# Subtractions with a higher priority, a scan whose vector and scalar instructions keep program order, and steps spread over more slots

## The chip, the cores and the metric

The kernel runs on one core of a Trainium2 chip. The metric is the device time of one execution in microseconds (us). Engines are named as in the profile: PE (matmul; PEld is its loading of weights), DVE (vector), ACT (scalar), POOL, SP (here it only issues DMAs).

## The reference

Two layers of a mixer over 256 tokens of 2048 features, in float32. One input projection feeds two groups of heads; both are gated and go through one output projection.

```
for l in range(DEPTH):
    h = rms_norm(x, norm_g[l])
    proj = jnp.einsum('btd,dc->btc', h, w_in[l])
    rw_in, g_rw, q, k_at, v_at, g_at = jnp.split(proj, col_splits, axis=-1)
    rw_in = bidir_token_shift(rw_in, shift_mu[l])
    r, k, v, xw, xa = jnp.split(rw_in, rw_splits, axis=-1)
    y_rw = rwkv7_branch(r, k, v, xw, xa, w0[l], decay_up[l], ...)
    ...                                   # rope on q and k
    y_at = window_attention(qh, kh, vh, sink[l])
    mix = concatenate([y_rw * silu(g_rw), y_at * silu(g_at)])
    x = x + jnp.einsum('btc,cd->btd', mix, w_out[l])
return rms_norm(x, final_g)
```

`rwkv7_branch` is a recurrence over time with a 64x64 state per head, run forward and backward for 16 heads, followed by a normalisation per head. `window_attention` has 16 heads over 4 key heads and a band of 128 tokens.

## The kernel before

**The matrix products.** Weights come as tiles of 128 x 1024 (half of 2048 rows times 128 output columns). `wload` (L205) issues one DMA into a `raw` buffer, of which there are three. `wsplit` (L210) makes two tiles of it, in two halves of 512 columns each: ACT copies raw to `hi` in the matmul's rounded format (L215), then DVE computes `lo = raw - hi` (L216). `hi` and `lo` have two buffers each. A `gemm` (L273 to L275) has 16 steps, eight a tile, each of three matmuls: activations' high part times `hi` (L273), their low part times `hi` (L274), their high part times `lo` (L275). `Stream.run(n)` issues n such steps, and asks for the next weight tile two steps before the last one ends. When a product is complete, an evacuation runs (`shift_evac` L400 to L403, `silu_evac` L411 to L413, rope L495 to L501).

**The recurrence.** Heads go in eight pairs p. Each pair passes three Python generators, which issue a part of their work at every `yield`:

- `scan_p` prepares: decays and rates through tanh (L645, L648), a scan along time (L658), exponentials `pp` and `ip` (L664, L665), a reciprocal of the key norm (L667), and the tiles `mv` (L675, L676, L690) and `bk` (L684, L687).
- `scan_i` makes and inverts a triangular matrix: a product masked into `ge` (L726), a half-precision copy `AB` (L735) and its remainder `AL` (L766), then six levels of products whose results are merged into `tv` and `tt` under a mask (L824, L825, for levels 1 to 5). Key rows are copied over a part of `ge` at L773.
- `scan_b` runs four steps along time: products into `pcc` (L870 from the second step on, L883, L893), an ACT copy to `suv` (L888), a DVE product into `suv` (L895). Its tail normalises over DVE, ACT and POOL (L911 to L915), and `mix_split` (L613) makes the high and low parts `MH`, `ML` of the result.

**What sets the order.** `window(64, ...)` cuts 64 gemm steps into 14 slots. In each slot the generators advance first, as the lists `STAGE_P`, `STAGE_I`, `STAGE_B` say (slot numbers; a number that stands twice means two advances), then four or five gemm steps are issued. Twelve windows make up most of a layer. In window w, `scan_p` works on pair w-1, `scan_i` on w-2 and w-3, `scan_b` on w-3 and w-4, so windows 3 to 8 have all three at once. Values of the attention are projected in window 8, keys and queries (rope) from window 9 on.

On PE the order is that of the program (L136). DVE, ACT and SP are ordered by a scheduler, which takes among the instructions that its own model holds ready the one of highest priority; priority falls in the order in which the code issues, and `scan_b` stands 95 places ahead (`PRIO_B`). Each engine then runs its list strictly in order.

**Buffers.** PSUM gives two tiles of two banks to all the scans' products (`wpair`), two banks to the gemms (`pm`), and one each to `pcc` and `py`.

Of the kernel before, what the change touches and what calls it, by code (L numbers as in the profile page):

```python
# [21 lines left out]
T = 256  # L22
# [15 lines left out]
NSH = 26  # L38
# [17 lines left out]

# [72 lines left out]
def hybrid_trunk_kernel(ctx, tc, xT, wi, wv, wo, par, fing, dup, iup, sink, pos, cst, out):  # L129
# [17 lines left out]
    def wpair(name):  # L147

        return ps_w.tile([128, 2, 512], F32, tag="w", name=name)
# [55 lines left out]
    def wload(src):  # L205
        raw = wrp.tile([128, 1024], F32, tag="raw", name="raw")
        SY.dma_start(out=raw, in_=src)
        return raw

    def wsplit(raw):  # L210
        hi = wsp.tile([128, 1024], F32R, tag="hi", name="hi")
        lo = wsp.tile([128, 1024], F32R, tag="lo", name="lo")
        for i in range(2):
            q = slice(i * 512, (i + 1) * 512)
            A.activation(hi[:, q], raw[:, q], AF.Copy)  # L215
            V.tensor_tensor(lo[:, q], raw[:, q], hi[:, q].bitcast(F32), op=ALU.subtract)  # L216
        return hi, lo

    def halves(src, first=None):
        return [lambda: wsplit(first if first is not None else wload(src[0])), lambda: wsplit(wload(src[1]))]  # L220

    class Stream:

# [383 lines left out]
    def layer(l):  # L607
# [21 lines left out]
                PE.matmul(o[r, 0:T], bones[r, r], x[r, 0:T], start=True, stop=True)  # L629


        def scan_p(p, t):
            K, VV, R, iu, du = t["k"], t["v"], t["r"], t["iu"], t["du"]
            dd = lambda x: x.rearrange("p (d x) -> p d x", d=2)
            two = lambda x: x.unsqueeze(1).to_broadcast([128, 2, T])
            c8 = lambda x: x.rearrange("p (n j) -> p n j", j=64)

            pza = wpair("pza")
            pz, pa = pza[:, 0], pza[:, 1]
            for d in range(2):  # L640
                low_rank(pz[:, d * T : (d + 1) * T], [a[0 : RANK + 1, d, :] for a in du], [a[0 : RANK + 1] for a in L.TW])
# [3 lines left out]
            A.activation(LW, pz, AF.Tanh, scale=0.5)  # L645
            TH = st("th", [2 * T])
            for d in range(2):
                A.activation(TH[:, d * T : (d + 1) * T], pa[:, d * T : (d + 1) * T], AF.Tanh, scale=0.5, bias=dpm(NSH + 16, d * 8 + p))  # L648
            sq = st("t1", [T], bufs=3)
            A.activation(sq, K, AF.Square, scale=prm(P_KK, p))  # L650
            KR = st("kkr", [T])
            A.activation(KR, K, AF.Identity, scale=prm(P_KK, p))
            yield

            V.tensor_scalar(LW, LW, 1.0, None, op0=ALU.add)
            msk = MSK.rearrange("p c j -> p (c j)")
            for x in (LW[:, 0:T], LW[:, T : 2 * T][:, ::-1]):
                V.tensor_tensor_scan(x, msk, x, 0.0, op0=ALU.mult, op1=ALU.add)  # L658
# [5 lines left out]
            A.activation(PP.rearrange("p d c j -> p (d c j)"), LW, AF.Exp, scale=DECAY_C)  # L664
            A.activation(IP.rearrange("p d c j -> p (d c j)"), LW, AF.Exp, scale=-DECAY_C)  # L665
            KD = st("kd", [T])
            V.reciprocal(KD, pk[:, 0:T])  # L667
            V.scalar_tensor_tensor(KD, KD, 1e24, KR, op0=ALU.min, op1=ALU.mult)
# [6 lines left out]
            V.scalar_tensor_tensor(MV[:, 0, :, 0, 1:64], PP[:, 0, :, 0:63], -1.0, kr4[:, :, 1:64], op0=ALU.mult, op1=ALU.mult)  # L675
            V.scalar_tensor_tensor(MV[:, 1, :, 0, 0:63], PP[:, 1, :, 1:64], -1.0, kr4[:, :, 0:63], op0=ALU.mult, op1=ALU.mult)  # L676
            A.activation(MV[:, 0, :, 0, 0:1], kr4[:, :, 0:1], AF.Copy, scale=-1.0)
            A.activation(MV[:, 1, :, 0, 63:64], kr4[:, :, 63:64], AF.Copy, scale=-1.0)
            A.activation(km, TH, AF.Identity, scale=dpm(NSH, p), bias=dpm(NSH + 8, p))
            yield  # L680
            V.scalar_tensor_tensor(dd(TH), dd(TH), 1.0, two(KD), op0=ALU.add, op1=ALU.mult)
            BK8 = BK.rearrange("p d c s j -> p (d c) s j")
            IP8 = IP.rearrange("p d c j -> p (d c) j")
            V.scalar_tensor_tensor(BK8[:, :, 1, :], c8(TH), 0.5, IP8, op0=ALU.mult, op1=ALU.mult)  # L684
            yield
            V.tensor_tensor(dd(km), dd(km), two(K), op=ALU.mult)
            V.tensor_tensor(BK8[:, :, 2, :], c8(km), IP8, op=ALU.mult)  # L687
            A.activation(BK8[64:128, :, 0, :], BK8[64:128, :, 2, :], AF.Copy)
# [5 lines left out]
            A.activation(PC[:, 0, :], PP[:, 0, :, 63], AF.Copy)  # L694
            A.activation(PC[:, 1, :], PP[:, 1, :, 0], AF.Copy)
            yield


            V.tensor_tensor(km[:, 0:T], km[:, 0:T], km[:, T : 2 * T], op=ALU.add)
            V.scalar_tensor_tensor(km[:, 0:T], km[:, 0:T], prm(P_RK, p), R, op0=ALU.mult, op1=ALU.mult)  # L700
            yield
            pb = wbank("pbn")
            head_sums(pb, km)
            bv = st("bv", [T], bufs=3)
            V.tensor_tensor(bv, pb[:, 0:T], VV, op=ALU.mult)
            t.update(BK=BK, MV=MV, PC=PC, bv=bv)
            yield


        def scan_i(p, t):  # L710
# [48 lines left out]
            for h in range(2):  # L759
                for q in range(2):  # L760
# [1 line left out]
                        pick(SUV, half[1 - h], q * 128 + h * 64, [NC * 128, 2], [256, 2], [1, 64]),  # L762
                        pts[h][half[q], 384:512].rearrange("p (b x) -> p b x", b=2).unsqueeze(1).to_broadcast([64, 2, 2, 64]), AF.Copy,
                    )
            for h in range(2):
                V.tensor_tensor(  # L766
                    flat(AL[half[h]]), GE[h][half[h]].rearrange("p d c s j -> p (d c) s j")[:, :, 0, :], flat(AB[half[h]]), op=ALU.subtract
                )


            for h in range(2):
                c3 = lambda x: pick(x, half[h], 0, [NC * 128 - 128, 2], [128, 3], [1, 64])
                A.activation(c3(GE[h][:, 0, 1:NC].rearrange("p c s j -> p (c s j)")), c3(MV[:, 0, 1:NC].rearrange("p c s j -> p (c s j)")), AF.Copy)  # L773

# [17 lines left out]
            for li, b in enumerate(LEVELS):  # L792
# [61 lines left out]
        def scan_b(p, t):  # L854
# [288 lines left out]
```

## Time and profile before

| | |
|---|---|
| time, three runs | 1252.38, 1253.78, 1256.28 us (median 1253.78) |
| profiled execution | 1253.19 us, span of the profile 1251.3 us |
| granted PE clock, mean | 0.993 of full speed |
| PE busy | 1186.6 us (95%), 16204 instructions |
| DVE busy | 928.8 us (74%), 2067 instructions |
| ACT busy | 747.3 us (60%), 1838 instructions |
| POOL busy | 19.0 us, 23 instructions |

The times are of unprofiled executions, the profile is of a further one. The trace can be asked for one engine's instructions in order of time; each row has the start and the length in us, the engine, the line, the operation, output and inputs with their shapes, and in brackets how long the engine stood idle ahead of it and what released it. `[0.84 <-ACT suv L888]` on a PE row says that PE stood for 0.84 us, until the ACT instruction that writes `suv` at L888 was done. Views by waits and by lines add such rows up. DVE lists its masked copies at L824 and L825 as CAST_PREDICATED in the trace and as COPY_PREDICATED in the program.

### The profile page before, as it was taken

What the parts mean: (1) busy time and instruction counts of PE and PEld (TensorE: products, weight loads), DVE (VectorE), ACT (ScalarE), POOL (GpSimd) and SP (SyncE); (2) the same over time, 40 slices, a digit from 0 to 9 for tenths busy, and PEclk for the clock granted to TensorE, in tenths of its full rate; (3) what the DMA queues carried; (4) which work ended last, traced back from release to release, by engine and by line L of the source; (5) the groups of instructions that cost most, each with busy time, mean ns of one, the idle gap of its engine ahead of it and who ended that gap; (6) DMA issues with size and microseconds to landing.
All of it is one profiled execution on the core that took longest, in us unless ns stands there. A gap on an engine that the chain in (4) does not pass through costs nothing. (4 is left out here: it accounts for less than half of the span.)

```text
span 1251.3 us, 38155 instructions
## 1 busy us (share of the span) xinstructions
PE 1186.6 (95%) x16204; PEld 1094.6 (87%) x16204; DVE 928.8 (74%) x2067; ACT 747.3 (60%) x1838; POOL 19.0 (2%) x23
## 2 busy tenths in 40 slices
PE   6989999999999999999999999999999999999996
PEld 6978888888888889999998888888888888899996
DVE  7878878887886668856676878878887766786654
ACT  6556665666566566645555655665666565665553
POOL 0000000000000000000000000000000000000000
PEclk9999999999999999999999999999999999999998
DMA  7443233322323434466654433223322333335663
GB/s 246 158 141 124 96 103 109 103 83 102 120 86 97 135 110 141 140 216 230 202 186 141 135 124 116 89 92 110 103 92 92 118 107 124 134 132 173 209 192 119
DMA packets 60411, 166.72 MB, mean 133 GB/s; under 512 B 7728, under 2 KB 22736, under 8 KB 60240
## 3 DMA queue, kind: packets, MB, share of 16 engines
q1 hardware_dynamic: 60240, 164.27, 39.9%
q8 instruction: 127, 2.08, 0.7%
q14 instruction: 44, 0.36, 0.1%
HBM read 157.43 MB, written 4.19 MB: 129 GB/s over the span
## 5 line engine op out<-in xcount | busy, mean ns | idle before, releaser
L273 PE MATMUL pm<-XH,hi 128*128 128x256 f32 x1664 | 495.9, 298 | 13.9 <-ACT XH L178 6.4
L275 PE MATMUL pm<-XH,lo 128*128 128x256 f32 x1664 | 470.6, 283 | 20.0 <-DVE lo L216 19.9
L274 PE MATMUL pm<-XL,hi 128*128 128x256 f32 x1664 | 468.6, 282 | 0.1
L215 ACT ACTIVATE hi<-raw 128x512 fp32r<-128x512 f32 x560 | 326.7, 624 | 201.6 <-PE pm L274 163.1
L216 DVE TENSOR_TENSOR lo<-raw,hi 128x512 fp32r<-128x512 f32 x560 | 367.8, 685 | 104.1 <-ACT hi L215 95.7
L273 PEld LDWEIGHTS pm<-XH,hi 128*128 128x128 f32 x1664 | 314.5, 189 | 40.0 <-issue 13.0
L275 PEld LDWEIGHTS pm<-XH,lo 128*128 128x128 f32 x1664 | 315.1, 189 | 25.7 <-DVE lo L216 25.6
L274 PEld LDWEIGHTS pm<-XL,hi 128*128 128x128 f32 x1664 | 315.0, 189 | 0.8 <-DVE XL L179 0.8
L273 PE MATMUL pm<-MH,hi 128*128 128x256 f32 x512 | 144.8, 283 | 1.6 <-ACT hi L215 1.6
L275 PE MATMUL pm<-MH,lo 128*128 128x256 f32 x512 | 144.6, 282 | 0.4 <-DVE lo L216 0.4
L274 PE MATMUL pm<-ML,hi 128*128 128x256 f32 x512 | 144.5, 282 | 0.0
L273 PEld LDWEIGHTS pm<-MH,hi 128*128 128x128 f32 x512 | 97.4, 190 | 2.6 <-ACT hi L215 1.8
L275 PEld LDWEIGHTS pm<-MH,lo 128*128 128x128 f32 x512 | 97.3, 190 | 0.6 <-DVE lo L216 0.6
L274 PEld LDWEIGHTS pm<-ML,hi 128*128 128x128 f32 x512 | 97.3, 190 | 0.0
L888 ACT ACTIVATE suv<-pcc 64x128 f32<-64x128 f32 x128 | 34.4, 269 | 16.2 <-PE pq L815 10.9
L968 ACT ACTIVATE mv<-mv,mx 128x257 f32<-128x257 f32 x64 | 31.9, 503 | 16.3 <-DVE mx L965 16.2
L726 DVE TENSOR_TENSOR ge<-pg,C 128x1024 f32<-128x1024 f32 x32 | 39.0, 1218 | 3.0 <-PE pg L720 3.0
L735 ACT ACTIVATE AB<-ge 64x512 f16<-64x512 f32 x32 | 20.1, 629 | 30.9 <-DVE ge L726 30.5
L720 PE MATMUL pg<-mv,bk 64*128 64x128 f32 x512 | 37.2, 285 | 0.0
L824 DVE CAST_PREDICATED tv<-LV,pd 128x256 f16<-128x256 uint8 x80 | 34.1, 426 | 1.7 <-PE pd L823 1.2
L817 ACT ACTIVATE QF<-pq 128x256 f16<-128x256 f32 x80 | 30.9, 386 | 6.9 <-PE pq L815 5.9
L825 DVE CAST_PREDICATED tt<-LV,pd 128x256 f16<-128x256 uint8 x80 | 34.0, 424 | 0.0
(240 smaller groups left out, 1843.6 us busy)
## 6 DMA issues: line engine op xcount, KB each, us to landing
raw<-wi SPq DMA_DIRECT2D x207, 512.0 KB, 3.4
raw<-wo SPq DMA_DIRECT2D x64, 512.0 KB, 3.3
raw<-wv SPq DMA_DIRECT2D x8, 512.0 KB, 3.2
rrot<-u SPq DMA_DIRECT2D x80, 32.0 KB, 1.9
vg<-xT SPq DMA_DIRECT2D x16, 128.0 KB, 4.1
xd<-vg SPq DMA_DIRECT2D x16, 128.0 KB, 3.3
vg<-xd SPq DMA_DIRECT2D x16, 128.0 KB, 3.3
g<-dup SPq DMA_DIRECT2D x16, 97.0 KB
```

Of the source, the lines that this page charges most:

```text
L215: A.activation(hi[:, q], raw[:, q], AF.Copy)
L216: V.tensor_tensor(lo[:, q], raw[:, q], hi[:, q].bitcast(F32), op=ALU.subtract)
L273: PE.matmul(pm, wh, rh[:, kk, :], start=(kk == 0), stop=False)
L274: PE.matmul(pm, wh, rl[:, kk, :], start=False, stop=False)
L275: PE.matmul(pm, wl, rh[:, kk, :], start=False, stop=(kk == 15))
L720: PE.matmul(pg[:, h, c * 128 : (c + 1) * 128], BK[half[h], d, c, 1 - h : 3 - h, :].rearrange("p s j -> p (s j)"), MV[half[h], d, c].rearra ...
L726: V.tensor_tensor(GEd(d), pg.rearrange("p h (c x) -> p h c x", c=NC), gm[d].unsqueeze(1).unsqueeze(1).to_broadcast([128, 2, NC, 128]), op= ...
L817: A.activation(t_sub(QF), flat4(pq[:, :, 0:128]), AF.Copy)
L824: V.copy_predicated(t_sub(TC), t_mask, flat4(pd[:, :, 0:128]))
L825: V.copy_predicated(v_sub(TT), v_mask, flat4(pd[:, 0, 128:384].rearrange("p (d x) -> p d x", d=2)))
L888: A.activation(here(h), pc[half[h], 1], AF.Copy)
L968: A.activation(Sc[:, h, q, 0:257], Sc[:, h, q, 0:257], AF.Exp, scale=0.125, bias=mx[:, q : q + 1], accum_out=den[:, q : q + 1])
```

## The change

Five things are edited.

1. In `wsplit` the subtraction is issued with a priority 40 places higher (`PRIO_LO`).
2. A wrapper `InTurn` makes each instruction that is called through it keep its place in the program's order on its engine: it stays behind the instruction issued before it there. All of `scan_p`'s ACT and DVE instructions go through it (`PA`, `PV`), and in `scan_i` and `scan_b` the copies `AB`, `AL`, the key rows, and most of the tail.
3. In `scan_i` the two `AB` copies are issued after a `yield` instead of before it, so one slot later; `AL` and the key rows are issued at level 1 and level 2 of the inversion instead of before level 0, which with `STAGE_I` is slot 4 and slot 6 instead of slot 2.
4. `scan_b`'s tail: the product with the gate is written in place instead of into `mf`, and there are three more `yield`s.
5. The second list of `STAGE_B` grows from `[1]` to `[1, 2, 3, 4]`, so that the tail's steps fall into slots 1 to 4 of the next window.

```
-STAGE_B = (list(range(1, 14)), [1])
+STAGE_B = (list(range(1, 14)), [1, 2, 3, 4])
...
+PRIO_LO = 40
...
-            V.tensor_tensor(lo[:, q], raw[:, q], hi[:, q].bitcast(F32), op=ALU.subtract)
+            with tc.high_priority(offset=PRIO_LO):
+                V.tensor_tensor(lo[:, q], raw[:, q], hi[:, q].bitcast(F32), op=ALU.subtract)
...
+    class InTurn:
...
+        def __getattr__(self, name):
+            return lambda *a, **k: tc.keep_in_program_order(getattr(self.engine, name)(*a, **k))
+
+    PA, PV = InTurn(A), InTurn(V)
...
         def scan_p(p, t):
...
-            V.tensor_scalar(LW, LW, 1.0, None, op0=ALU.add)
+            PV.tensor_scalar(LW, LW, 1.0, None, op0=ALU.add)
...
             for h in range(2):
-                A.activation(flat(AB[half[h]]), GE[h][half[h]].rearrange("p d c s j -> p (d c) s j")[:, :, 0, :], AF.Copy)
-            yield
+                PA.activation(flat(AB[half[h]]), GE[h][half[h]].rearrange("p d c s j -> p (d c) s j")[:, :, 0, :], AF.Copy)
...
-            for h in range(2):
-                V.tensor_tensor(
-                    flat(AL[half[h]]), GE[h][half[h]].rearrange("p d c s j -> p (d c) s j")[:, :, 0, :], flat(AB[half[h]]), op=ALU.subtract
-                )
...
+            def low_rows():
+                for h in range(2):
+                    PV.tensor_tensor(
...
+            def key_rows():
...
                 pq = wpair("pq")
+                if li in (1, 2):
+                    (low_rows, key_rows)[li - 1]()
                 if li == 0:
...
-            V.tensor_tensor(ysq, py, yv.unsqueeze(2).to_broadcast([128, NC, 64]), op=ALU.mult)
+            PV.tensor_tensor(ysq, py, yv.unsqueeze(2).to_broadcast([128, NC, 64]), op=ALU.mult)
...
             A.activation(Zt, pz, AF.Identity, scale=prm(P_LG, p), bias=prm(P_LB, p))
-            V.tensor_tensor(Zt, Zt, bv, op=ALU.add)
-            mix_split(p, Zt, t["gr"])
+            yield
+            PV.tensor_tensor(Zt, Zt, bv, op=ALU.add)
+            PV.scalar_tensor_tensor(Zt, Zt, 0.5, t["gr"], op0=ALU.mult, op1=ALU.mult)
+            yield
+            PA.activation(MH[:, p, :], Zt, AF.Copy)
+            yield
+            PV.tensor_tensor(ML[:, p, :], Zt, MH[:, p, :].bitcast(F32), op=ALU.subtract)
             yield
```

The number of instructions stays as it was on every engine. PE's order does not change, nor POOL's; on SP two weight loads come behind the four small copies of a rope step in two places. What moves is the order on DVE and ACT. Three places of it follow, as the program's lists have them (line, operation, output and inputs, shape; x2 stands for two in a row). Lines of the changed kernel lie somewhat further down: L216 of before is L218, L215 is L216, L824 is L844, L888 is L908, L895 is L915, L400 to L403 are L413 to L416, and every instruction that goes through the wrapper is listed under the wrapper's own line, L231.

**ACT, slots 5 and 6 of a window with all three scans.** Names: `pp`, `ip` exponentials of `scan_p`, `suv` of `scan_b`, `ge<-mv` key rows. Before:

```order
L645 ACTIVATE lw<-pza 128x512
L648 ACTIVATE th<-pza,DP 128x256 x2
L664 ACTIVATE pp<-lw 128x512
L888 ACTIVATE suv<-pcc 64x2x64 x2
L665 ACTIVATE ip<-lw 128x512
L694 ACTIVATE pc<-pp 128x4
L695 ACTIVATE pc<-pp 128x4
L679 ACTIVATE lw<-th,DP 128x512
L215 ACTIVATE hi<-raw 128x512 x2
```

Now:

```order
L231 ACTIVATE lw<-pza 128x512
L231 ACTIVATE th<-pza,DP 128x256 x2
L231 ACTIVATE t_3813<-kr,PR 128x256
L231 ACTIVATE kkr<-kr,PR 128x256
L231 ACTIVATE ge<-mv 64x6x64
L908 ACTIVATE suv<-pcc 64x2x64 x2
L231 ACTIVATE ge<-mv 64x6x64
L216 ACTIVATE hi<-raw 128x512 x2
L837 ACTIVATE QF<-pq 128x2x32x4
L231 ACTIVATE pp<-lw 128x512
L231 ACTIVATE ip<-lw 128x512
```

The `suv` copies leave the place behind `pp` and now stand behind two small ACT instructions and one key-row copy; `pp` and `ip` come behind two `hi` copies and a merge copy.

**DVE, slots 6 to 8 of the same window.** `kd`, `th`, `bk` and `mv` are `scan_p`'s, `vg` and `u` an evacuation's, `tv` and `tt` `scan_i`'s. Before:

```order
L667 RECIPROCAL kd<-pk 128x256
L216 TENSOR_TENSOR lo<-raw,hi 128x512
L668 SCALAR_TENSOR_TENSOR kd<-kd,kkr 128x256
L400 TENSOR_TENSOR u<-pm,rb 128x256
L824 COPY_PREDICATED tv<-LV,pd 128x2x32x4
L825 COPY_PREDICATED tt<-LV,pd 128x2x32x4
L402 SCALAR_TENSOR_TENSOR vg<-u,PR,vg 128x255
L681 SCALAR_TENSOR_TENSOR th<-th,kd 128x512
L403 SCALAR_TENSOR_TENSOR vg<-u,PR,vg 128x255
L684 SCALAR_TENSOR_TENSOR bk<-th,ip 128x8x64
L216 TENSOR_TENSOR lo<-raw,hi 128x512 x2
L687 TENSOR_TENSOR bk<-lw,ip 128x8x64
```

Now:

```order
L231 SCALAR_TENSOR_TENSOR kd<-kd,kkr 128x256
L844 COPY_PREDICATED tv<-LV,pd 128x2x32x4
L845 COPY_PREDICATED tt<-LV,pd 128x2x32x4
L231 SCALAR_TENSOR_TENSOR mv<-pp,kkr 128x4x63
L415 SCALAR_TENSOR_TENSOR vg<-u,PR,vg 128x255
L231 SCALAR_TENSOR_TENSOR mv<-pp,kkr 128x4x63
L416 SCALAR_TENSOR_TENSOR vg<-u,PR,vg 128x255
L218 TENSOR_TENSOR lo<-raw,hi 128x512 x2
L231 SCALAR_TENSOR_TENSOR th<-th,kd 128x512
L231 SCALAR_TENSOR_TENSOR bk<-th,ip 128x8x64
```

The pair of `lo` comes ahead of `th` and `bk`; the two `mv` products, which stood ahead of slot 6's work, now stand here.

**DVE, slots 3 to 5 of window 9, layer 0, where rope is computed.** `u`, `rrot` and `iu` are the rope's. Before:

```order
L496 TENSOR_TENSOR u<-u,TW 128x256
L497 TENSOR_TENSOR rrot<-rrot,XA 128x256
L895 TENSOR_TENSOR suv<-pcc,pc 64x2x64
L498 TENSOR_TENSOR u<-u,rrot 128x256
L895 TENSOR_TENSOR suv<-pcc,pc 64x2x64
L216 TENSOR_TENSOR lo<-raw,hi 128x512
L501 TENSOR_TENSOR iu<-u,kr 128x256
```

Now:

```order
L509 TENSOR_TENSOR u<-u,TW 128x256
L510 TENSOR_TENSOR rrot<-rrot,XA 128x256
L845 COPY_PREDICATED tt<-LV,pd 128x2x64x2
L511 TENSOR_TENSOR u<-u,rrot 128x256
L218 TENSOR_TENSOR lo<-raw,hi 128x512
L915 TENSOR_TENSOR suv<-pcc,pc 64x2x64
L514 TENSOR_TENSOR iu<-u,kr 128x256
L231 TENSOR_TENSOR ML<-t_7134,MH 128x256
L915 TENSOR_TENSOR suv<-pcc,pc 64x2x64
L231 TENSOR_TENSOR AL<-ge,AB 64x512 x2
```

A masked copy, a `lo`, a rope product and the tail's `ML` come to stand among or ahead of the two `suv` products.

More of the change, by code (lines that the diff above doesn't have):

```diff
@@ L663, in scan_p @@
             IP = st("ip", [2, NC, 64])
-            A.activation(PP.rearrange("p d c j -> p (d c j)"), LW, AF.Exp, scale=DECAY_C)
-            A.activation(IP.rearrange("p d c j -> p (d c j)"), LW, AF.Exp, scale=-DECAY_C)
+            PA.activation(PP.rearrange("p d c j -> p (d c j)"), LW, AF.Exp, scale=DECAY_C)
+            PA.activation(IP.rearrange("p d c j -> p (d c j)"), LW, AF.Exp, scale=-DECAY_C)
             KD = st("kd", [T])
-            V.reciprocal(KD, pk[:, 0:T])
-            V.scalar_tensor_tensor(KD, KD, 1e24, KR, op0=ALU.min, op1=ALU.mult)
+            PV.reciprocal(KD, pk[:, 0:T])
+            PV.scalar_tensor_tensor(KD, KD, 1e24, KR, op0=ALU.min, op1=ALU.mult)
             yield
@@ L674, in scan_p @@
             kr4 = KR.rearrange("p (c j) -> p c j", j=64)
[L675 to L679, printed above, removed]
+            PV.scalar_tensor_tensor(MV[:, 0, :, 0, 1:64], PP[:, 0, :, 0:63], -1.0, kr4[:, :, 1:64], op0=ALU.mult, op1=ALU.mult)
+            PV.scalar_tensor_tensor(MV[:, 1, :, 0, 0:63], PP[:, 1, :, 1:64], -1.0, kr4[:, :, 0:63], op0=ALU.mult, op1=ALU.mult)
+            PA.activation(MV[:, 0, :, 0, 0:1], kr4[:, :, 0:1], AF.Copy, scale=-1.0)
+            PA.activation(MV[:, 1, :, 0, 63:64], kr4[:, :, 63:64], AF.Copy, scale=-1.0)
+            PA.activation(km, TH, AF.Identity, scale=dpm(NSH, p), bias=dpm(NSH + 8, p))
             yield
-            V.scalar_tensor_tensor(dd(TH), dd(TH), 1.0, two(KD), op0=ALU.add, op1=ALU.mult)
+            PV.scalar_tensor_tensor(dd(TH), dd(TH), 1.0, two(KD), op0=ALU.add, op1=ALU.mult)
             BK8 = BK.rearrange("p d c s j -> p (d c) s j")
             IP8 = IP.rearrange("p d c j -> p (d c) j")
-            V.scalar_tensor_tensor(BK8[:, :, 1, :], c8(TH), 0.5, IP8, op0=ALU.mult, op1=ALU.mult)
+            PV.scalar_tensor_tensor(BK8[:, :, 1, :], c8(TH), 0.5, IP8, op0=ALU.mult, op1=ALU.mult)
             yield
-            V.tensor_tensor(dd(km), dd(km), two(K), op=ALU.mult)
-            V.tensor_tensor(BK8[:, :, 2, :], c8(km), IP8, op=ALU.mult)
-            A.activation(BK8[64:128, :, 0, :], BK8[64:128, :, 2, :], AF.Copy)
+            PV.tensor_tensor(dd(km), dd(km), two(K), op=ALU.mult)
+            PV.tensor_tensor(BK8[:, :, 2, :], c8(km), IP8, op=ALU.mult)
+            PA.activation(BK8[64:128, :, 0, :], BK8[64:128, :, 2, :], AF.Copy)
             yield
-            V.tensor_tensor(
+            PV.tensor_tensor(
                 MV[:, :, :, 1, :], R.rearrange("p (c j) -> p c j", j=64).unsqueeze(1).to_broadcast([128, 2, NC, 64]), PP, op=ALU.mult
@@ L693, in scan_p @@
             PC = st("pc", [2, NC], bufs=3)
[L694 to L695 removed]
+            PA.activation(PC[:, 0, :], PP[:, 0, :, 63], AF.Copy)
+            PA.activation(PC[:, 1, :], PP[:, 1, :, 0], AF.Copy)
             yield
[L699 to L700 removed]
+            PV.tensor_tensor(km[:, 0:T], km[:, 0:T], km[:, T : 2 * T], op=ALU.add)
+            PV.scalar_tensor_tensor(km[:, 0:T], km[:, 0:T], prm(P_RK, p), R, op0=ALU.mult, op1=ALU.mult)
             yield
@@ L764, in scan_i @@
                     )
-            for h in range(2):
-                V.tensor_tensor(
-                    flat(AL[half[h]]), GE[h][half[h]].rearrange("p d c s j -> p (d c) s j")[:, :, 0, :], flat(AB[half[h]]), op=ALU.subtract
-                )
-            for h in range(2):
-                c3 = lambda x: pick(x, half[h], 0, [NC * 128 - 128, 2], [128, 3], [1, 64])
-                A.activation(c3(GE[h][:, 0, 1:NC].rearrange("p c s j -> p (c s j)")), c3(MV[:, 0, 1:NC].rearrange("p c s j -> p (c s j)")), AF.Copy)
+            def low_rows():
+                for h in range(2):
+                    PV.tensor_tensor(
+                        flat(AL[half[h]]), GE[h][half[h]].rearrange("p d c s j -> p (d c) s j")[:, :, 0, :], flat(AB[half[h]]), op=ALU.subtract
+                    )
+            def key_rows():
+                for h in range(2):
+                    c3 = lambda x: pick(x, half[h], 0, [NC * 128 - 128, 2], [128, 3], [1, 64])
+                    PA.activation(
+                        c3(GE[h][:, 0, 1:NC].rearrange("p c s j -> p (c s j)")), c3(MV[:, 0, 1:NC].rearrange("p c s j -> p (c s j)")), AF.Copy
+                    )
             TC = st("tv", [2, NC, 64], F16)
```

15 lines of the change are left out of this document (9 added, 6 removed).

## The prediction

> **What bounds the kernel now.** I read the busy line first, then PE's waits, then where they lie in time. This is the page's line of the engines:
>
> ```profile
> PE 1186.6 (95%) x16204; PEld 1094.6 (87%) x16204; DVE 928.8 (74%) x2067; ACT 747.3 (60%) x1838; POOL 19.0 (2%) x23
> ```
>
> PE is the bound, and with 1251.3 us of span it is idle for 64.7 us. The stretches below (length, then busy time of PE, PEld, DVE, ACT, POOL; clock, DMA share, GB/s) are a whole period of the recurrence, a piece of the output projection, and the end:
>
> ```profile
> 205.13:249.39 44.26, 42.49 (x756) 38.27 (x756) 35.48 (x74) 28.34 (x74) 1.01 (x2) 1.00 0.30 102
> 600.00:640.00 40.00, 40.00 (x340) 40.00 (x340) 26.03 (x51) 20.03 (x40) 0.70 (x1) 1.00 0.61 196
> 1240.00:1252.00 12.00, 1.20 (x4) 0.93 (x4) 5.18 (x7) 0.38 (x1) 0.54 (x1) 0.54 0.44 175
> ```
>
> The end costs 10.8 us (12.00 - 1.20) that no part of the change touches. In the period PE stands 1.77 us; in the pure projection not at all. Who PE waits for (sum, times, longest):
>
> ```profile
> PE pm L275 <- DVE lo L216: 20.3, 27, 1.6
> PE pcc L893 <- ACT suv L888: 10.0, 11, 1.7
> PE pm L273 <- ACT XH L178: 6.4, 1, 6.4
> PE pm L273 <- ACT hi L215: 4.7, 4, 1.7
> PE pm L273 <- DVE VA L523: 3.1, 2, 1.6
> PE pf L831 <- DVE tv L824: 2.0, 2, 1.1
> PE pq L815 <- DVE tv L824: 1.9, 6, 0.4
> ```
>
> So 64.7 = 10.8 at the end + 6.4 at the first activations + about 47 of waits for DVE and ACT. That 47 caps what a new order can give. The two largest rows are nearly all one pattern, first and last of each in PE's rows (the bracket is the idle time):
>
> ```profile
> 109.69 0.39 PE L275 MATMUL pm<-XH,lo 128*128 128x256 f32 x1 [0.82 <-DVE lo L216]
> 185.26 0.45 PE L893 MATMUL pcc<-suv,bt 128*64 128x64 f32 x8 [0.84 <-ACT suv L888]
> 229.52 0.45 PE L893 MATMUL pcc<-suv,bt 128*64 128x64 f32 x8 [0.84 <-ACT suv L888]
> 239.35 0.39 PE L275 MATMUL pm<-XH,lo 128*128 128x256 f32 x1 [0.81 <-DVE lo L216]
> 929.82 0.45 PE L893 MATMUL pcc<-suv,bt 128*64 128x64 f32 x8 [0.85 <-ACT suv L888]
> 939.64 0.38 PE L275 MATMUL pm<-XH,lo 128*128 128x256 f32 x1 [0.81 <-DVE lo L216]
> ```
>
> The suv stall (slot 6) comes in windows 4 to 7 of both layers, 8 times; the lo stall (slot 8) in windows 2 to 7, 12 times.
>
> **The suv stall.** ACT's and DVE's rows of the period tell why it is there:
>
> ```profile
> 227.09 1.27 DVE L658 TENSOR_TENSOR_SCAN lw<-MSK,lw 128x256 f32<-128x256 f16 x2
> 228.40 0.63 ACT L664 ACTIVATE pp<-lw 128x512 f32<-128x512 f32 x1 [1.52 <-DVE lw L658]
> 228.93 0.54 ACT L888 ACTIVATE suv<-pcc 64x128 f32<-64x128 f32 x2
> ```
>
> ACT stands 1.52 us for the scan with `pp` at its head, and suv, which needs only PE, is queued behind. PE wants it at 229.52 - 0.84 = 228.68. In the new list suv has `t`, `kkr` and one key-row copy ahead, from 226.87 on (when the `th` pair ends): three copies of about 0.4 to 0.5 each, then suv's 0.54, so about 228.1 at the latest if I count all four in full. That is 0.6 ahead of need. I take the stall as gone: 8 x 0.84 = 6.7 us. Behind it a second wait lies hidden:
>
> ```profile
> 229.73 0.44 DVE L824 CAST_PREDICATED tv<-LV,pd 128x256 f16<-128x256 uint8 x1
> 230.22 0.30 PE L815 MATMUL pq<-tv,AB 64*64 64x32 f16 x16
> 230.64 0.65 PE L629 MATMUL pk<-t,C 64*64 64x256 f32 x4
> ```
>
> The merge ends at 230.17 and PE's product starts at 230.22 without a bracket. The merge stood behind two `mv` products that waited for `pp`; now it stands ahead of the scan and is done some 3 us sooner. For this I count between 0 and 0.4 us a window (230.64 - 230.22 is the nearest row), and take 0.2: 8 x 0.2 = 1.6 us.
>
> **The lo stall.** DVE's rows ahead of it:
>
> ```profile
> 233.01 1.76 DVE L667 RECIPROCAL kd<-pk 128x256 f32<-128x256 f32 x1
> 237.01 0.69 DVE L681 SCALAR_TENSOR_TENSOR th<-th,kd 128x512 f32<-128x512 f32 x1
> 238.01 0.68 DVE L684 SCALAR_TENSOR_TENSOR bk<-th,ip 128x512 f32<-128x512 f32 x1
> 238.62 1.28 DVE L216 TENSOR_TENSOR lo<-raw,hi 128x512 fp32r<-128x512 f32 x2
> 233.19 0.63 ACT L215 ACTIVATE hi<-raw 128x512 fp32r<-128x512 f32 x1 [0.71 <-PE pm L274]
> ```
>
> The `hi` was there 4 us before its `lo`: only DVE's order held it. The pair now overtakes `th` and `bk`. One such operation takes 0.61 from start to start here (238.01 to 238.62), so 1.22 is won; the two `mv` products that come in ahead of it cost some 0.7; and `mv` and `lw` products left the stretch between slot 5 and slot 7 (two long ones, 1.2, and the idle time for `pp`, 0.7), against which the two `AL` come in from slot 2 (1.2). On balance the pair starts 1.2 - 0.7 + 1.9 - 1.2 = 1.2 us sooner, at 237.4, and its first half is done at 238.0. PE wants it at 239.35 - 0.81 = 238.5 by its old clock, but comes 0.84 + 0.2 sooner in the windows with the suv stall: 237.5. By this crude sum 0.5 of 0.81 would stay; walking the list operation by operation, with what each waits for, I get 236.8 at the latest and no stall. I take 0.1 left on average: 12 x 0.71 = 8.5 us. The bounds are 12 x 0.3 = 3.6 and 12 x 0.82 = 9.8.
>
> **The single stalls.** They have these rows:
>
> ```profile
> 52.12 0.39 PE L275 MATMUL pm<-XH,lo 128*128 128x256 f32 x1 [1.18 <-DVE lo L216]
> 75.01 0.39 PE L275 MATMUL pm<-XH,lo 128*128 128x256 f32 x1 [1.58 <-DVE lo L216]
> 367.34 0.38 PE L273 MATMUL pm<-XH,hi 128*128 128x256 f32 x1 [1.55 <-DVE VA L523]
> 979.08 0.38 PE L273 MATMUL pm<-XH,hi 128*128 128x256 f32 x1 [1.55 <-DVE VA L523]
> ```
>
> At 52.12 the `lo` was queued behind the angle arithmetic of the set-up; with its priority it goes one place ahead: I take 1.0 of 1.18 (bounds 0 and 1.2). In window 8 the evacuation `VA` is queued behind the reciprocal, which starts sooner because two long products and the wait for `pp` have left the place ahead of it (1.9 us by the same operations as above, 1.55 wanted): I take 1.3 each, 2.6 together (bounds 2.0 and 3.1). In window 1 it goes both ways: the `lo` at 75.01 gains a place or two, but ACT now puts two `hi` copies behind `pp` and `ip` (1.1 us), where one stood ahead. I take +0.5 for each layer, bounds -2 and +1.5: 1.0 together.
>
> **Where it costs.** In windows 9 and 10 rope, tail and inversion meet, and the order turns against `scan_b`:
>
> ```profile
> 397.55 0.45 PE L893 MATMUL pcc<-suv,bt 128*64 128x64 f32 x8 [1.67 <-ACT suv L888]
> 410.20 0.45 PE L870 MATMUL pcc<-suv,ge 128*64 128x64 f32 x8 [0.52 <-DVE suv L895]
> 408.45 0.42 DVE L496 TENSOR_TENSOR u<-u,TW 128x256 f32<-128x256 f32 x1 [1.38 <-DMA rrot<-u]
> ```
>
> At 410.20 PE waits for the `suv` pair that stands among the rope's products, which wait for a DMA. Now a masked copy and a `lo` come ahead of the pair's first half, a rope product and `ML` between the halves: 0.33 + 0.60 + 0.33 = 1.3 us by starts of their like, and 0.33 of the old order comes off. I take +1.5 in layer 0 and +1.0 in layer 1. Against that, suv at 397.55 and its twin in layer 1 lose about 0.7 each by the same cause as above. Four merges in slots 13 and 0 have a `lo` or two ahead of them that they had not: 0.3 to 0.6 each, 1.8 together. Net: -2.5 + 1.4 - 1.8 = -2.9 us; bounds -7 and 0.
>
> The DMAs are the same ones; two weight loads go behind four rope copies, and nothing in PE's list of waits names a load, so I cost that at nothing (if the three raw buffers did not cover it, 3.4 us of a load's landing would show at most twice).
>
> **The sum.** 6.7 + 1.6 + 8.5 + 1.0 + 2.6 + 1.0 - 2.9 = 18.5. The profiled execution took 1253.19 us, 1.89 above its span, which I leave as they are: 1253.2 - 18.5 = 1234.7. The median of the three runs lies 0.6 above the profiled one, well below what I can resolve. Two terms have more room above than below (the hidden wait and the lo stalls), so I say **1234 us**. All terms at their best give 6.7 + 3.2 + 9.8 + 1.2 + 3.1 + 3.0 = 27.0 (1226), all at their worst 6.7 + 0 + 3.6 + 0 + 2.0 - 4 - 7 = 1.3 (1252). They lie at different places and will hardly all fall one way, so the forecast's own range is 1227 to 1244.
>
> **Rivals.** *DVE becomes the bound in slot 12.* With the low parts ahead, the level-4 merge stands behind two `lo` and two products of an evacuation:
>
> ```profile
> 246.52 0.42 DVE L824 CAST_PREDICATED tv<-LV,pd 128x256 f16<-128x256 uint8 x1
> 247.94 0.30 PE L815 MATMUL pq<-tv,AB 64*64 64x32 f16 x16
> ```
>
> It was done 1.0 us ahead of its use. PE now comes 1.9 sooner, and DVE must come as much sooner with it; by my walk 0.35 us are left. If the walk is off by 1.2, each of some 14 windows (2 to 8, both layers) pays 0.85: 12 us given back, 1246. Against it: DVE is busy for 35.48 of 44.26, so it has the time; for it: it has hardly a pause in the middle of the window.
>
> *Slower: scan_p's pinned chain comes late.* `pp` now stands on ACT behind two `hi` and a merge copy; the pinned `mv` products on DVE wait for it, and behind these stand `vg`, the `lo` pair and `th`. By the rows `pp` should come near 231.5 and `mv` not be reached before 234.5, so 3 us are spare. The `hi` copies wait for buffers, though:
>
> ```profile
> L215 ACT ACTIVATE hi<-raw 128x512 fp32r<-128x512 f32 x560 | 326.7, 624 | 201.6 <-PE pm L274 163.1
> L216 DVE TENSOR_TENSOR lo<-raw,hi 128x512 fp32r<-128x512 f32 x560 | 367.8, 685 | 104.1 <-ACT hi L215 95.7
> ```
>
> From 3 + 1.0 us of lateness on, the lo stall is back and grows one for one, and to be slower than before it must also eat the 1.9 of a window: over 5.9 us late. At 7 us, 12 x 1.1 = 13 us lost in steady windows against some 5 won elsewhere: about 1261.
>
> *Buffers, not order.* If `hi` and `lo` lack room, a higher priority cannot bring `lo` forward, and only the suv part is left: 1253 - 8 + 3 = 1248, or no change if that too is held by PSUM's two pairs. For it: 163.1 us of ACT's idle time before `hi` end with a matmul that frees a buffer. Against it: at 238.62 the `hi` had been ready for 4 us. [...] The row of 233.19 speaks against it here, so it gets a small chance.
>
> *More than the trace shows.* PEld stands 5.99 us in the period where PE stands 1.77, so some slack lies under overlapping matmuls, as with the merge at 229.73. If 0.5 more came free in each of 14 windows, it would be 7 us: 1227. [...]
>
> **How the numbers follow.** Forecast (1227 to 1244) 0.66; slot 12 gives back half 0.14; more than shown 0.06; buffers 0.08, of which 0.06 within 0.3%; pinned chain late 0.06, of which 0.04 slower and 0.02 near no change. A measurement of this kernel tells 0.3%, 3.8 us, from no change. Faster: 0.66 + 0.14 + 0.06 + 0.02 = 0.88; same 0.08; slower 0.04. The range for 8 in 10 takes in the forecast's bounds, most of the slot-12 case and a part of the larger gain: 1225 to 1247.
>
> **What would show it.** Right: no bracket for suv in slot 6 and none for `lo` in slot 8 of windows 2 to 7, a period near 42.4 instead of 44.26, PE's waits near 35, a `suv` wait above 1.5 in window 9. Wrong: brackets of `tv` at the inversion's products in slot 12 (first rival); `pp` or `mv` as releasers ahead of `lo` (second); `hi` just ahead of its `lo` with the bracket unchanged (third); a period below 42.0 (fourth).

## The result, and the profile after

The changed kernel takes 1235.4 us (median of 4 runs, 1234.25 to 1238.04) against 1254.72 us before; the ratio is 0.9851, 95% interval 0.9826 to 0.9875. The forecast was 1234 us. The profiled execution of the changed kernel took 1234.27 us, with a span of 1232.4 us, 18.9 us less than before. The engines' line of the page after:

```profile
PE 1182.2 (96%) x16204; PEld 1096.3 (89%) x16204; DVE 930.7 (76%) x2067; ACT 743.0 (60%) x1838; POOL 19.1 (2%) x23
```

PE's idle time is down from 64.7 to 50.2 us; the other 4.4 us came out of PE's busy time, which covers waits that overlapping matmuls hide (PE's rows of `pm` are 0.28 us long and start 0.12 us apart) and is longer where the clock drops (0.41 us and 0.21 us at half clock; last section). This is who PE waits for now, by its list of waits (sum, times, longest):

```profile
PE pm L286 <- ACT XH L179: 5.9, 1, 5.9
PE pbn L642 <- DVE lw L231: 5.6, 2, 2.8
PE pk L642 <- ACT t L231: 5.4, 2, 2.9
PE pm L288 <- DVE lo L218: 4.9, 7, 1.5
PE pf L851 <- DVE tt L845: 3.5, 2, 2.4
PE pq L835 <- DVE tv L844: 3.5, 4, 1.0
PE pf L851 <- DVE tv L844: 2.7, 2, 1.5
```

PE's wait for ACT's `suv` is gone but for 0.3 us, the wait for `lo` fell from 20.3 in 27 places to 4.9 in 7. Two rows are new, `pbn` and `pk`, and they are as large as anything that is left but the first activations (`XH`). The period of the recurrence in its stretch of time (length, busy time of PE, PEld, DVE, ACT, POOL; clock, DMA, GB/s):

```profile
204.21:246.21 42.00, 42.00 (x756) 38.12 (x755) 35.41 (x74) 27.83 (x74) 1.01 (x2) 1.00 0.34 109
```

It was 44.26 with 42.49 of PE busy; now PE does not stand at all. Of the 2.26 us, 1.65 were the brackets of the two stalls (0.84 and 0.81), and some 0.6 waits that PE's busy time had covered, or gaps too short for a bracket. These are the rows of the changed kernel for the two stalls; the first three are ACT's and DVE's, the others PE's:

```profile
225.92 0.55 ACT L908 ACTIVATE suv<-pcc 64x128 f32<-64x128 f32 x2
229.10 0.62 ACT L231 ACTIVATE pp<-lw 128x512 f32<-128x512 f32 x1
234.57 1.29 DVE L218 TENSOR_TENSOR lo<-raw,hi 128x512 fp32r<-128x512 f32 x2
227.78 0.45 PE L913 MATMUL pcc<-suv,bt 128*64 128x64 f32 x8
228.39 0.30 PE L835 MATMUL pq<-tv,AB 64*64 64x32 f16 x16
228.54 0.63 PE L642 MATMUL pk<-t,C 64*64 64x256 f32 x4
236.27 0.28 PE L288 MATMUL pm<-XH,lo 128*128 128x256 f32 x1
```

`suv` runs ahead of `pp`, and no PE row has a bracket. Set beside the same products before (229.52, 230.22, 230.64 and 239.35), the rows give the lead at each: 1.74, 1.83, 2.10 and 3.08 us.

PE runs the same instructions in the same order in both kernels, so the time of one matmul in both traces tells how far the changed kernel is ahead at that point. Such a product at the start of window 4 and of window 8, layer 0, in PE's rows before:

```profile
164.52 0.30 PE L831 MATMUL pf<-tv,NEYE 64*64 64x256 f16 x4
...
341.60 0.30 PE L831 MATMUL pf<-tv,NEYE 64*64 64x256 f16 x4
```

and after:

```profile
165.95 0.30 PE L851 MATMUL pf<-tv,NEYE 64*64 64x256 f16 x4
...
333.95 0.30 PE L851 MATMUL pf<-tv,NEYE 64*64 64x256 f16 x4
```

The changed kernel is 1.43 us behind at the first and 7.65 ahead at the last. Done for the whole program, with the products of the prediction's terms beside it:

| stretch | gained, measured | forecast |
|---|---|---|
| start to window 2, layer 0 | -3.7 | +1.5 |
| windows 2, 3, layer 0 | +2.3 | +1.4 |
| windows 4 to 7, layer 0 | +9.1 | +7.0 |
| window 8, layer 0 | -0.7 | +1.3 |
| window 9, layer 0, to window 1, layer 1 | +2.7 | -1.7 |
| window 1 from slot 4 on, layer 1 | -5.1 | +0.5 |
| windows 2, 3, layer 1 | +2.2 | +1.4 |
| windows 4 to 7, layer 1 | +9.1 | +7.0 |
| window 8, layer 1 | +0.5 | +1.3 |
| window 9, layer 1, to the end | +2.6 | -1.2 |
| sum, unrounded | 18.9 | 18.5 |

The sums agree; the terms don't. Windows 2 to 7 gave 5.8 us more than forecast and the late windows 8.2 more, and the starts of the layers came out 10.8 us worse and window 8 2.9 worse.

### The profile page after: what moved, and what is told of

The parts are those of the page before. It is cut to its first block, busy times and chain, and to the rows that moved or that the text cites. A ratio compares the mean times of both kernels' runs of the same rounds, so it can differ in the third digit from the quotient of the medians.

```text
span 1232.4 us, 38183 instructions
## 1 busy us (share of the span) xinstructions
PE 1182.2 (96%) x16204; PEld 1096.3 (89%) x16204; DVE 930.7 (76%) x2067; ACT 743.0 (60%) x1838; POOL 19.1 (2%) x23
## 5 line engine op out<-in xcount | busy, mean ns | idle before, releaser
L216 ACT ACTIVATE hi<-raw 128x512 fp32r<-128x512 f32 x560 | 328.1, 625 | 238.0 <-PE pm L287 147.9
L218 DVE TENSOR_TENSOR lo<-raw,hi 128x512 fp32r<-128x512 f32 x560 | 368.4, 687 | 96.7 <-ACT hi L216 89.2
L288 PEld LDWEIGHTS pm<-XH,lo 128*128 128x128 f32 x1664 | 318.3, 191 | 6.5 <-DVE lo L218 6.4
L287 PEld LDWEIGHTS pm<-XL,hi 128*128 128x128 f32 x1664 | 318.3, 191 | 0.9 <-DVE XL L180 0.9
L908 ACT ACTIVATE suv<-pcc 64x128 f32<-64x128 f32 x128 | 34.2, 267 | 18.1 <-PE pq L835 11.8
L837 ACT ACTIVATE QF<-pq 128x256 f16<-128x256 f32 x80 | 30.8, 385 | 19.8 <-PE pq L835 19.0
L844 DVE CAST_PREDICATED tv<-LV,pd 128x256 f16<-128x256 uint8 x80 | 34.4, 430 | 7.7 <-PE pd L843 6.9
L892 ACT ACTIVATE rh<-pcc 128x128 f32<-128x128 f32 x64 | 17.5, 273 | 35.4 <-PE pcc L890 35.0
```

Of the source, the lines that this page charges most:

```text
L287: PE.matmul(pm, wh, rl[:, kk, :], start=False, stop=False)
L288: PE.matmul(pm, wl, rh[:, kk, :], start=False, stop=(kk == 15))
L837: A.activation(t_sub(QF), flat4(pq[:, :, 0:128]), AF.Copy)
L844: V.copy_predicated(t_sub(TC), t_mask, flat4(pd[:, :, 0:128]))
L908: A.activation(here(h), pc[half[h], 1], AF.Copy)
```

## Experiments

All times are medians beside the kernel before on the same chip (1254.7, 1256.1 and 1254.4 us in the three groups); the brackets hold the 95% interval of the ratio.

**The priority alone** (kernel before, one edit):

```
+PRIO_LO = 40
-            V.tensor_tensor(lo[:, q], raw[:, q], hi[:, q].bitcast(F32), op=ALU.subtract)
+            with tc.high_priority(offset=PRIO_LO):
+                V.tensor_tensor(lo[:, q], raw[:, q], hi[:, q].bitcast(F32), op=ALU.subtract)
```

> Only the higher priority of the low parts, in the kernel before. Theory A (two stalls with a cause each: DVE's order for lo, ACT's order for suv): the lo stall of 0.82 in slot 8 goes, the suv stall of 0.84 in slot 6 stays, the period falls from 44.27 to about 43.45, and the time to about 1245. Theory B (the engines as a whole are late, an edit alone only moves the wait): period stays near 44.2, time 1252 to 1255. PE's waits for lo in windows 2 to 7 decide: none by A, other releasers of the same size by B.

1252.5 us, ratio 0.9985 [0.997, 1.0]: nothing to speak of, and the time is where theory B had it. PE's rows of a steady window in that run:

```profile
229.95 0.45 PE L895 MATMUL pcc<-suv,bt 128*64 128x64 f32 x8 [0.85 <-ACT suv L890]
242.60 0.30 PE L817 MATMUL pq<-tv,AB 64*64 64x32 f16 x16 [0.43 <-DVE tv L826]
```

The lo stall of slot 8 is gone, as theory A said, but a stall of 0.43 for a merge, in slot 10, eats half of it (the kind of the prediction's first rival, in a kernel without the pins); the period is 43.7. The rest went at other places: new waits of 1.67 and 1.51 us for `lw` in window 1, larger ones in window 9.

**The change without the priority:**

```
-PRIO_LO = 40
+PRIO_LO = 0
```

> The changed kernel without the higher priority of the low parts (pins and spread stay). Theory A: suv stall gone, lo stall of 0.8 back in 12 windows, period 42.8, and against the changed kernel 12 x 0.8 = 10 us more: 1245. Theory B: period 44.2, time 1252 or more. A third reading, that the pins alone give the low parts their place (scan_p's products are held back by their pins): period 42.0, 1235, and the priority does nothing.

1228.9 us, ratio 0.9793 [0.9762, 0.9823]: faster than the change by 6.5 us, which no reading had foreseen: the third had the period (42.0), but said that the priority does nothing. The period:

```profile
202.28:244.18 41.90, 41.90 (x756) 38.02 (x756) 35.29 (x74) 27.79 (x74) 1.01 (x2) 1.00 0.33 107
```

No lo stall comes back in windows 3 to 7 with `lo` at its old priority. (In window 2 of each layer `lo` costs 1.1 us again, in two waits, where the changed kernel waits 0.96 for a merge.) Theory A, and with it the prediction's reading of the lo stall, fell here.

**The change without scan_p's pins** (`A` and `V` for `PA` and `PV` inside `scan_p`; the other pins and the priority stay):

```
-            PA.activation(LW, pz, AF.Tanh, scale=0.5)
+            A.activation(LW, pz, AF.Tanh, scale=0.5)
...
```

> The changed kernel with scan_p's ACT and DVE instructions free again; the priority, the spread and the other pins stay. Theory A: pp is back ahead of suv on ACT, the suv stall of 0.84 and the hidden wait of the merge come back in windows 4 to 7, period 43.1 to 43.2, against the changed kernel 8 x 1.1 = 9 us more there. In window 1 the square of k can run early again, so the wait of pk (2.9 and 2.4 us) and half-clock stretches behind it should go: 5 to 9 us less. Together 1235 to 1240. Theory B: the pins carry nothing, period 42.0, and only the window 1 part shows: 1227 to 1230.

1234.8 us, ratio 0.984 [0.9818, 0.9861], the time of the change. The suv stall did not come back, against theory A. In ACT's rows of that run the two key-row copies and `suv` still run ahead of `pp`:

```profile
223.13 1.05 ACT L231 ACTIVATE ge<-mv 64x384 f32<-64x384 f32 x2
224.19 0.55 ACT L908 ACTIVATE suv<-pcc 64x128 f32<-64x128 f32 x2
225.54 0.63 ACT L678 ACTIVATE pp<-lw 128x512 f32<-128x512 f32 x1 [0.80 <-DVE lw L672]
```

So the change repairs that stall twice, once by `scan_p`'s pins and once by the rest of it. Without any pin and without the priority `pp` is back ahead of `suv` (the run with only the spread, below). The pinned key rows are the likely second repair, but no run tests them apart from the other pins and the priority. A merge wait of 0.3 stays in the period (42.3). The wait of `pk` in window 1 is gone (5.4 us in all); against it stand more waits for `VA` (3.2 after 0.5), `lo` (7.4 after 4.9) and `hi` (5.2 after 2.6), and a sixth stretch of half clock (last section) where the changed kernel has five.

**Only scan_p's pins, in the kernel before:**

```
-            A.activation(LW, pz, AF.Tanh, scale=0.5)
+            PA.activation(LW, pz, AF.Tanh, scale=0.5)
...
-            V.reciprocal(KD, pk[:, 0:T])
+            PV.reciprocal(KD, pk[:, 0:T])
...
```

> The kernel before with one thing of the change: scan_p's ACT and DVE instructions keep program order. No priority, no spread of AB, AL, key rows and tail. New theory E (the pins of scan_p carry both repairs: pp leaves its place ahead of suv on ACT, and the products that follow pp come later on DVE, so that lo stands in time): period 42.0 to 42.2, no lo stall in slot 8 and no suv stall in slot 6, time 1228 to 1232, like the changed kernel without the priority. Rival F (spread and pins are needed together): a stall of 0.4 or more per period stays, period over 42.4, time over 1236.

1234.2 us, ratio 0.9834 [0.9813, 0.9855]. The period:

```profile
201.41:243.33 41.92, 41.92 (x756) 38.05 (x756) 35.15 (x74) 28.01 (x74) 1.01 (x2) 1.00 0.33 107
```

Both stalls are gone with this one part: theory E holds for the steady windows, and rival F, which expected a rest in the period, is wrong there. In time the run lies between the two, above E's 1232 and below F's 1236. It is some 5 us behind the change without the priority (by ratios, 0.0041 of 1255; 0.0028 by the repeat of that run below, with intervals that overlap). What is left of the old waits lies in window 9: 1.44 and 2.57 us for `suv`. In the change without the priority the first is gone and 0.18 stays of the second, so the spread or the other pins remove them.

**Only the spread** (change without priority and without any pin):

```
-    PA, PV = InTurn(A), InTurn(V)
+    PA, PV = A, V
...
-PRIO_LO = 40
+PRIO_LO = 0
```

> The changed kernel without any pin and without the priority: AB, AL, the key rows and the tail are issued in their new slots, nothing else. Theory E: pp stands ahead of suv again and two lo behind bk, so both stalls of 0.8 are back, period 43.8 to 44.3, time 1247 to 1254. Rival F: period 43.0 to 43.5 since the spread alone frees DVE at slot 2, time 1240 to 1246.

1251.8 us, ratio 0.9969 [0.9955, 0.9983]. PE's rows of a steady window:

```profile
229.43 0.45 PE L913 MATMUL pcc<-suv,bt 128*64 128x64 f32 x8 [0.44 <-ACT suv L908]
239.26 0.38 PE L288 MATMUL pm<-XH,lo 128*128 128x256 f32 x1 [0.81 <-DVE lo L218]
```

The lo stall is all there, half of the suv stall too; the period is 43.86. As theory E said, the spread alone is worth little.

**Window 1: is it the load?** The two new rows of PE's waits lie in window 1 of both layers. ACT's rows of the changed kernel there:

```profile
66.70 0.42 ACT L455 ACTIVATE duh<-g 97x256 fp32r<-97x256 f32 x1 [4.38 <-DMA g<-dup]
...
67.80 0.82 ACT L231 ACTIVATE th<-pza,DP 128x256 f32<-128x256 f32 x2
68.52 0.50 ACT L231 ACTIVATE t<-kr,PR 128x256 f32<-128x256 f32 x1
```

PE's wait for it, and the second new one:

```profile
69.07 0.65 PE L642 MATMUL pk<-t,C 64*64 64x256 f32 x4 [2.92 <-ACT t L231]
85.59 0.65 PE L642 MATMUL pbn<-lw,C 64*64 64x256 f32 x4 [2.77 <-DVE lw L231]
```

ACT stands 4.38 us for a small load whose buffer, the ring `g`, is held by the silu evacuation. Before the change ACT stood as long, but the square `t` of this pair was done long ahead of it, and `pk` waited for nothing, as the rows of before show:

```profile
39.00 0.49 ACT L650 ACTIVATE t<-kr,PR 128x256 f32<-128x256 f32 x1
```

```profile
64.48 0.65 PE L629 MATMUL pk<-t,C 64*64 64x256 f32 x4
```

```profile
65.00 0.42 ACT L442 ACTIVATE duh<-g 97x256 fp32r<-97x256 f32 x1 [4.33 <-DMA g<-dup]
```

Now `t` is pinned behind `th`, and that is queued behind the load. In the first attempt all pairs' loads got two tiles that are idle in those windows:

```
-                    t[n] = st("g", [2, 128], bufs=2)
+                    t[n] = st("dg" if n == "du" else "mf", [2, 128])
```

> The changed kernel, with the small weight tiles iup and dup loaded into two tiles that are idle there instead of the ring g they share with the silu evacuation, so that their loads are issued some six weight loads earlier. Theory C (window 1's new waits come from ACT and DVE standing 4 us for this load, with scan_p's square of k pinned behind it): the waits of pk (2.9, 2.4) and of pbn (2.8, 2.8) go, and with them two or three stretches of half clock that cost 1.7 us each: 1219 to 1224. Theory D (window 1 is bound by DVE's work, low parts ahead of scan_p): DVE starts earlier but PE still waits for pbn; 1230 to 1235.

1229.1 us, ratio 0.9798 [0.9772, 0.9824], between the two theories: the wait of `pk` is gone, that of `pbn` stayed (3.19 and 2.78), and loads that now wait for `dg` and `mf` at the start of a layer hold up weight loads behind them (waits for `hi` of 1.30 and 2.77 us). So only the second pair, with free tiles, and without the priority:

```
-                    t[n] = st("g", [2, 128], bufs=2)
+                    t[n] = st("dg" if n == "du" else "ysq", [2, 128]) if p == 1 else st("g", [2, 128], bufs=2)
```

> The changed kernel without the priority, and with iup and dup of the second pair alone loaded into two tiles idle there (of the other pairs, as before, into the ring g), so that the load no SP queue has to wait for is early and the weight loads at the start of a layer keep their places. Theory C: the waits of window 1 in the run without the priority (pk 3.0 and 2.6, lo 1.4 and 1.4, pbn 0.9 and 2.1) and two half-clock stretches of 1.7 each go, 1228.9 - 11 to 15 = 1214 to 1218. Theory D (window 1 is bound by DVE's work): pk's wait goes but pbn or lo waits as long, 1224 to 1229.

1221.2 us, ratio 0.9725 [0.9702, 0.9748], again between C and D. By ratios it is 8.5 us below the change without the priority. PE's waits there:

```profile
PE pm L288 <- DVE lo L218: 8.1, 12, 1.4
PE pm L286 <- ACT XH L179: 6.2, 1, 6.2
PE pbn L642 <- DVE lw L231: 3.0, 2, 2.1
```

No row of `pk` is left; `pbn` still waits 0.86 and 2.14, a `lo` in window 1 still 1.40. The load caused the first wait (C); what is left waits for DVE's own products, with the load in time (D).

> The kernel before with scan_p's instructions in program order and the second pair's iup and dup loaded early; none of the rest of the change. Theory E with C: as the run without the priority and with the early load, within 3 us: 1214 to 1221. Rival F: 8 us or more above that run.

That kernel (`scan_p`'s pins and the early load, nothing else of the change) took 1224.9 us, ratio 0.9765 [0.9745, 0.9785], 3.8 us above the last on the same chip: a little more than the 3 us that E and C gave it, and far from F's 8.

**Does the priority cost, or was it chance?** Four kernels on one chip: the change with twice the priority, the change, the change without it, and the fastest one.

> The changed kernel with the low parts 80 places ahead instead of 40. Theory G (the priority repairs nothing that the pins have not repaired, and takes DVE from scan_p, the merges and the tail where DVE is late: windows 1, 2, 9 and 10): more of it costs more. Waits of pbn in window 1 of 2.8 each or more, of tv and tt in windows 2, 8, 9 and 10 above the 10 us that the changed kernel has there; 2 to 10 us above the changed kernel. Rival H (the 6.5 us between the changed kernel and the one without the priority are chance, from where the half-clock stretches fall): within 2 us of the changed kernel.

> The changed kernel itself, on one chip with the next two. Theory G: 1235, 6 to 7 us above the one without the priority. Rival H: less than 3 us above it.

> The changed kernel without the priority, again, beside the changed kernel on one chip. Theory G: 1228 to 1230, 6 to 7 us below the changed kernel. Rival H: less than 3 us below it.

> The fastest so far, again: the changed kernel without the priority and with the second pair's iup and dup loaded early. Theory C: 7 to 8 us below the one without the priority on the same chip, 1219 to 1222, faster than both kernels. If that distance was chance: less than 4 us.

| kernel | us, median | ratio to before |
|---|---|---|
| priority 80 | 1238.3 | 0.9861 [0.9843, 0.988] |
| the change (40) | 1236.2 | 0.9844 [0.9821, 0.9866] |
| no priority | 1231.2 | 0.9806 [0.9786, 0.9826] |
| no priority, early load | 1221.4 | 0.9732 [0.9713, 0.9751] |

The change is 5.0 us above the one without the priority here, 6.5 in the first group. That is theory G's side of the line, but the intervals still touch, so the size is loose. Between 40 and 80 the times can't be told apart, so that more of it costs more time is not shown; the waits of window 1 can, by PE's rows with 80:

```profile
67.44 1.06 PE L642 MATMUL pk<-t,C 64*64 64x256 f32 x4 [4.12 <-ACT t L231]
84.84 1.12 PE L642 MATMUL pbn<-lw,C 64*64 64x256 f32 x4 [3.63 <-DVE lw L231]
```

The `pbn` wait of layer 0 is 0.86 with priority 0, 2.77 with 40 and 3.63 with 80 (layer 1: 2.15, 2.78, 3.25). Between `pk` and the product that PE wants, DVE runs 9 low parts in layer 0 with priority 0 and 10 with 40, which fits; with 80 there are 10 as well, so the last step has another cause, left open. The early load is worth 9.7 us here; this kernel is faster than both kernels of the case.

## Why the prediction was right, and where its steps were not

- **What bounds the kernel.** Right: PE, with waits for DVE's and ACT's order. The wait for the first activations stays (5.9 after 6.4 us).
- **The suv stall, 6.7 us.** Right: it is gone in all eight windows, `suv` no longer stands behind `pp`. That the change without `scan_p`'s pins would do the same was not foreseen. The margin was added up wrongly: from 226.87, three copies of 0.4 to 0.5 and 0.54 end at 228.6 to 228.9, about when PE wanted `suv` (228.68), not at 228.1. In the trace it ends at 226.47, 1.3 us ahead of 227.78, because the `th` pair ends 2.06 us sooner (224.81), which the sum did not have.
- **The hidden wait behind it, 1.6 us.** The mechanism was right, the size too small. Between the `suv` product and `pk` the lead grows from 1.74 to 2.10: 0.36, where 0.2 were taken and 0.4 given as the bound. The rest of the 0.6 a window lies at the two stalls themselves, which gave 0.90 and 0.98 (2.10 to 3.08) where the brackets said 0.84 and 0.81. That is the nearest rival of the forecast, "more than the trace shows"; the period of 42.00 stands at the line that was drawn for it.
- **The lo stall, 8.5 us.** The gain was right, and slightly low (no bracket is left where 0.1 was kept). Its cause was not: the step "the pair now overtakes `th` and `bk`" credited the priority, which proved not to be needed there. Counted from the same matmul at the start of the period, the pair starts at 33.4 us before, at 32.2 with the priority alone (the 1.2 of the sum), at 30.8 with `scan_p`'s pins alone and at 30.2 with the whole change; PE takes it at 31.9. What moved `lo` far enough is the other half of that same sum, the `mv` and `lw` products and the wait for `pp` that left the stretch ahead, and these are moved by `scan_p`'s pins. Nor were the two largest rows "nearly all one pattern": 12 x 0.82 is 9.8 of the 20.3 us for `lo`. The rest fell as well, by some 5.6 us, mostly in window 1, where the waits of `pk` and `pbn` took its place.
- **The single stalls.** `VA` gained 1.3 twice, as said. At 52.12, 1.0 of 1.18 was said and about 0.3 came: 0.22 stays there, and 0.70 appears at a `lo` some 2.4 us behind it. And the wait for `tt` at the end of window 8 grew from 0.43 to 2.43 and from 0.25 to 1.10, since a `lo` more stands ahead of the merge, behind the rope's DMA (DVE stands 2.19 us for it); without the priority it is 1.50 and 0.24. This was not in the sum. The step on window 1 failed: "I take +0.5 for each layer, bounds -2 and +1.5". It looked at `lo` and `hi` there and not at what the pins put behind the load of `dup`. With `pk` (2.92, 2.43), `pbn` (2.77, 2.78) and four more stretches of half clock (last section; some 1.5 us each), the starts of the layers cost 8.8 us where 2.0 were to be won.
- **Where it costs.** Mis-sized, with the wrong sign: -2.9 was said for windows 9 and 10, and from window 9 on both layers gained, 5.3 together. The losses that were named came in part (`suv` at 410.20 went from 0.52 to 1.28, a merge behind it from 0.20 to 0.57), but more of the old waits went (`suv` at 397.55 lost all its 1.67, 0.7 was said), and a stretch of half clock at the layer's end (at 558) did not come again, which was in no term: the wait ahead of it is still there, 1.22 after 1.59.
- **The first rival, slot 12.** It came in window 2 of both layers, 0.96 us each, and not in windows 3 to 7; with the priority alone a merge of slot 10 waited 0.43 in each of these. DVE's margin was narrow, as said.
- **Buffers.** Excluded: with the same buffers and order of loads, PE stands for nothing in the period (42.00 us busy of 42.00); the repeated waits of 0.8 us came from the order of two queues.
- **The signs.** No bracket for `suv` in slot 6 nor for `lo` in slot 8 of windows 2 to 7: right. PE's list of waits adds up to 40.7 us where 35 was said, the longest `suv` wait of window 9 is 1.28 where one above 1.5 was said, and the period is 42.00 where 42.4 was said.

The total was right by luck: errors of 14 us up and 14 us down cancelled.

## What to carry to other kernels

Where a stall repeats, ask which instruction at the head of a queue is waiting, and take that one out of the place; raising the priority of what is queued behind it moved the wait (0.82 became 0.43) and took time where the engine was late anyway. A chain that is held to program order hides its cost where its first input is late, at the start of a phase rather than in the steady state: look there for what it now stands behind, loads included. And compare two kernels with one order on PE by the time of the same matmul in both traces: it gives the gain of each stretch, hidden waits and clock with it.

## What the runs showed of the hardware

Stalls cost more than their brackets where the granted clock fell from 1.00 to 0.50 behind them. Around `pk` in the changed kernel, three stretches (columns as above; the clock is the 1.00 and 0.50 ahead of the DMA share):

```profile
67.10:70.51 3.41, 1.44 (x11) 1.06 (x12) 3.33 (x7) 2.85 (x8) 0.00 (x0) 1.00 0.03 11
70.51:73.92 3.41, 3.41 (x18) 3.41 (x18) 3.32 (x6) 3.41 (x9) 0.00 (x0) 0.50 0.00 0
73.92:77.33 3.41, 3.41 (x31) 3.41 (x31) 3.41 (x8) 1.75 (x4) 0.00 (x0) 1.00 0.82 268
```

PE was busy for 1.44 of 3.41 us, and in the next 3.41 us it had half its clock: 18 matmuls where 31 fit afterwards. In the profiles of the kernel before and of the changed kernel such stretches last 3.41 us (but for the program's end, where PE stops), and within one run their starts lie whole numbers of such stretches apart (15.90, 29.55, 70.51, 674.67 and 688.32 in the changed kernel). Counted on from those starts, and from 10 us to 1200 us, the full-clock stretches ahead of a half-clock one had PE busy for 1.52 and 1.45 us in the kernel before and for 1.84, 1.70, 1.44, 1.93 and 0.71 us in the changed one. Three others of 1.74 to 1.97 us before, and three of 1.95 to 1.99 us in the changed kernel, had full clock behind them. In a second profile of the changed kernel (its run of the four on one chip) one stretch, from 666.9 to 673.7 us, is double; PE was busy for 2.9 us of its first half. The stretch at 29.55 costs 1.5 us: its 16 matmuls took 3.37 us, and 1.88 in the kernel before. The kernel before has two such stretches, the changed one five before its last matmuls; three more at 1.5 us each are 4.5 us, by estimate, of what its steady windows won. The second profile, with three of them, one double, took 1230.6 us. Of the changed kernel's ten executions the fastest (1230.6 us) had a mean granted clock of 0.991 and the slowest (1238.9 us) one of 0.985: 0.006 of 1235 us is 7.4 us, so by this estimate most of the spread goes with the clock, though not in every execution (1236.5 us also had 0.985). Since a stretch with PE busy for 1.93 us had half clock behind it and one with 1.74 us did not, no single stall can be priced with it beforehand.
